# Modulation products in four column groups, a layer norm's normalisation on ScalarE, and a different rhythm of offering its steps

## The chip, the core and the metric

One core of one Trainium2 chip runs the whole program. The metric is the device time of one execution in microseconds. The core has TensorE (PE in the profile), VectorE (DVE), ScalarE (ACT), GpSimd (POOL), and SyncE (SP), which here only issues DMAs. Instructions of one engine run in program order, and an instruction waits on semaphores for what it reads.

## What is computed

One layer of a hybrid block over 1024 tokens and 256 context tokens, D = 2048. Only its first part matters here:

```
m = silu(c) @ w_ada + b_ada                  # shift, scale, gate; 3 x 2048; also for c_ctx
h  = layernorm(x)  * (1 + scale)  + shift    # x: 1024 x 2048
hc = layernorm(xc) * (1 + scale_c) + shift_c # context: 256 x 2048
z  = h @ w_in ;  zc = hc @ w_in              # 6400 columns, cut into the branches
# then an S5 scan, a pooling branch, an RWKV-7 scan, gates, and
x_new = layernorm(alpha * x + gate * (merged @ w_out)) * ln_g + ln_b
```

All of it is in float32. The product `silu(c) @ w_ada` has two rows, one for c and one for c_ctx.

## The kernel before

`phase_ab` computes everything up to the S5 and pooling branches, and `phase_c` the RWKV scan and the output. `phase_ab` has two parts: `adaln` (the first stage) and `in_proj`.

**The first stage.** `adaln` cuts the shift and scale columns of `w_ada` into 128 pieces of 128 x 512 (256 KB each): 4 blocks of 512 columns, for each the scale part and then the shift part, for each part 16 pieces along the contraction. One loop at its end goes over the pieces. It keeps `ARAWS` = 7 pieces in flight through a ring of seven buffers (`ada_load`), and issues an x tile (128 x 2048, 1 MB) after every seventh loaded piece (`x_load`), all on SP's queue. For each piece one product is written: two columns of `sil` as stationary operand, the piece as the moving one, into two partitions of a PSUM tile `ps`. A float32 product is two instructions on PE. After 16 pieces `modulate` copies the two rows out on ACT (`row`), turns them into columns with four small products, and adds the bias on DVE.

**The layer norm.** `layernorm(t, line)` is a generator that runs between the pieces. For each of ten tiles (two of context first): four `bn_stats` and a `bn_aggr` on DVE, a square root on ACT, a reciprocal and the normalisation `(x - mean) * rstd` on DVE, then twice eight transposes on PE, each eight followed by four copies out of PSUM, taken by ACT and DVE in turn. Three such lines run interleaved (`LINES`).

**The operands of the projection.** When all ten tiles are normalised and a block's scale and shift are there, `modulate` goes on for that block: for each of its four groups of 128 features a multiply-add on DVE (`xT`), a rounding copy on ACT (`hi`), a remainder on DVE (`lo`), and the same for the context with two ACT instructions and one on POOL. So there are 16 such steps in all. `in_proj` then starts with feature block 48; it needs the first 256 features for its first step and the last ones for its last.

**What sets the order.** Nothing is scheduled at run time. While the program is written, `Clock` adds up a model of each engine: `note` prices every instruction (`COST` for the three elementwise engines, the number of columns for PE, bytes for DMA) and remembers when each tile is written and read. `Sched.tick(most)` is called between products; it takes up to `most` steps whose due time lies at or before the modelled time of PE, and writes their instructions at this place. `in_proj` uses the same `Sched` and the same `Clock` for all its side work (conv, norms, S5, pooling), with `tick(MOST)` after every projected group. So a price in `COST` changes the program order in all of `phase_ab`. `phase_c` has a planner of its own (`Pace`), which the change doesn't touch.

Most instructions of `phase_ab` are recorded under one line, L300, because a wrapper issues them; they are told apart by the tile names: `ada` (the PSUM tile of the products), `araw` (a piece), `x`, `pm` (transposes; later the projection), `row`, `misc`, `xT`, `hi`, `lo`, `xcT`, `hc_hi`, `hc_lo`. In the late phase, lines 2053 and 2059 are products of 128 rows by 64 columns whose outputs alternate between the two halves of PSUM's partitions: column-tiled products, two groups of 64 columns. Lines 2443 to 2445 are full 128 x 128 products beside them.

Of the kernel before, what the change touches and what calls it, by code (L numbers as in the profile page):

```python
# [9 lines left out]
FT = mybir.dt.float32  # L10
# [13 lines left out]
ALPHA = 2.0 ** 0.25  # L24
AHEAD = 3
ARAWS = 7
LINES = 3
RING = 20
QUOTA = 0.8
# [213 lines left out]
class Clock:  # L243


    LAT = {"tensor": 0.25, "scalar": 0.2, "vector": 0.15, "gpsimd": 0.15}
    COST = {"scalar": (0.17, 0.00075), "vector": (0.08, 0.00105), "gpsimd": (0.1, 0.0022)}

    def __init__(self):
        self.free = dict.fromkeys(("tensor", "scalar", "vector", "gpsimd", "sync", "hwdge", "dma"), 0.0)  # L250
# [3 lines left out]
    def note(self, eng, op, args, kw):  # L254
        aps = [x for x in (*args, *kw.values()) if isinstance(x, bass.AP)]
        if not aps:
            return
        out, ins = aps[0], aps[1:]
        n = math.prod(out.shape[1:])
        o = out.tensor.name  # L260
        who = "dma" if op == "dma_start" else eng
        marks = [self.written.get(x.tensor.name) for x in ins]
        if out.space != DRAM:
            marks += [self.written.get(o), self.read.get(o)]
            if o in self.before:
                p = self.before.pop(o)
                marks += [self.written.get(p), self.read.get(p)]
        t = max([self.free[eng]] + [m[1] for m in marks if m and (m[0] != who or who == "dma")])
        if who == "dma":
            self.free[eng] = t + (1.05 if eng == "gpsimd" else 0.05)  # L270
            t = self.free["hwdge"] = max(t, self.free["hwdge"]) + 0.45
            t = self.free["dma"] = max(t + 0.6, self.free["dma"]) + out.shape[0] * n * 4 / 360e3
            done = t + 1.0
        else:
            if eng == "tensor":
                cost = max(n, 64) * (1 if ins[0].dtype == FR else 2 if op == "transpose" else 4) / 2400
            else:
                a, b = self.COST[eng]
                cost = a + b * n
            t = self.free[eng] = t + cost  # L280
            done = t + self.LAT[eng]
        self.written[o] = who, done
        for x in ins:
            self.read[x.tensor.name] = who, done
        self.last = max(self.last, done)
# [230 lines left out]
def adaln(tc, A, g, const, hb, psA, ap_, raws, hc_hi, hc_lo):  # L516


    nc = tc.nc
    sched = Sched(tc.clock)  # L520
    order = (8, 9, 0, 1, 2, 3, 4, 5, 6, 7)
    x_t, normed = {}, []

    def x_load():
        t = order[len(x_t)]
        x_t[t] = hb.tile([128, D], FT, tag="hb", name=f"x{t}")
        nc.sync.dma_start(x_t[t], A["x"][0, t * 128:(t + 1) * 128, :] if t < 8 else A["ctx"][0, (t - 8) * 128:(t - 7) * 128, :])

    pieces = [(blk, part, k) for blk in range(4) for part in (1, 0) for k in range(16)]
    loaded = []  # L530

    def ada_load():
        blk, part, k = pieces[len(loaded)]
        r = raws.tile([128, 512], FT, name="araw")
        nc.sync.dma_start(r, A["w_ada"][0, k * 128:(k + 1) * 128, part * D + blk * 512:part * D + (blk + 1) * 512])
        loaded.append(r)

    x_load()
    cv, (oc, occ, ob) = load_cols(
        tc, A, g, ap_, psA,  # L540
        [(rows_of(A["c"], 16), 16), (rows_of(A["c_ctx"], 16), 16), (rows_of(A["b_ada"], 48), 48)], "cv")
    ada_load()
    x_load()
    g.sil = sil = const.tile([128, 16, 2], FT, name="sil")
    for i, o in enumerate((oc, occ)):
        nc.scalar.activation(sil[:, :, i], cv[:, o:o + 16], AF.Silu)
    xc_t = ap_.tile([128, 16, TC], FT, name="xcT")
    xT = []
    mod = ap_.tile([128, 16, 2, 2], FT, name="mod")

    def layernorm(t, line):
        while t not in x_t:
            yield
        xt = x_t[t]
        st = ap_.tile([128, 4, 6], FT, name=f"bst{line}", tag=f"bst{line}")
        mv = ap_.tile([128, 4], FT, name=f"mv{line}", tag=f"mv{line}")
        yield
        for i in range(4):
            nc.vector.bn_stats(st[:, i], xt[:, i * 512:(i + 1) * 512])
        nc.vector.bn_aggr(mv[:, 0:2], st)  # L560
        nc.vector.tensor_scalar(mv[:, 2:3], mv[:, 1:2], 1e-6, None, op0=OP.add)
        nc.scalar.activation(mv[:, 3:4], mv[:, 2:3], AF.Sqrt)
        yield
        nc.vector.reciprocal(mv[:, 2:3], mv[:, 3:4])
        nc.vector.tensor_scalar(xt, xt, mv[:, 0:1], mv[:, 2:3], op0=OP.subtract, op1=OP.mult)
        while t < 8 and not {8, 9} <= set(normed):
            yield
        if not xT and t < 8:
            xT.extend(hb.tile([128, 2, T], FT, tag="hb", name=f"xT{i}") for i in range(7))
            xT.append(ap_.tile([128, 2, T], FT, name="xT7"))  # L570
        yield
        for q in range(2):
            ps = psA.tile([128, 8, 128], FT, name="pm", tag="pm", bufs=2)
            for i in range(8):
                k = 8 * q + i
                nc.tensor.transpose(ps[:, i], xt[:, k * 128:(k + 1) * 128], g.ident)
            for b in range(4):
                i = 4 * q + b
                dst = xT[i][:, :, t * 128:(t + 1) * 128] if t < 8 else xc_t[:, 2 * i:2 * i + 2, (t - 8) * 128:(t - 7) * 128]
                copy_on(nc, "dve" if b % 2 else "act", dst, ps[:, 2 * b:2 * b + 2])  # L580
            yield
        normed.append(t)

    def lines(j):
        for t in order[j::LINES]:
            yield from layernorm(t, j)

    g.hi, g.lo, g.made = hi, lo, made = [], [], []

    def modulate(blk, part, ps):  # L590

        row = ap_.tile([2, 512], FT, name="row", tag="row")
        nc.scalar.activation(row, ps[0:2], AF.Copy)
        yield
        pt = psA.tile([128, 512], FT, name="misc", tag="misc", bufs=2)
        for i in range(4):
            nc.tensor.matmul(pt[:, 2 * i:2 * i + 2], row[0:2, i * 128:(i + 1) * 128], g.ident[0:2, 0:2], start=True, stop=True)
        b0 = ob + part * 16 + blk * 4
        m = mod[:, 4 * blk:4 * blk + 4, part, :]
        nc.vector.tensor_tensor(m, pt[:, 0:8].rearrange("p (k m) -> p k m", m=2),  # L600
                                cv[:, b0:b0 + 4].unsqueeze(2).to_broadcast([128, 4, 2]), op=OP.add)
        if part:
            nc.vector.tensor_scalar(m, m, 1.0, None, op0=OP.add)
            return
        yield
        while len(normed) < 10:
            yield
        while len(hi) < 2 * blk:
            yield
        for i in (2 * blk, 2 * blk + 1):  # L610
            h_hi = hb.tile([128, 2, T], FR, tag="hb", name=f"hi{i}")
            h_lo = hb.tile([128, 2, T], FR, tag="hb", name=f"lo{i}")
            hi.append(h_hi)
            lo.append(h_lo)
            for j in range(2):
                k = 2 * i + j
                x, xc = xT[i][:, j], xc_t[:, k]
                nc.vector.tensor_scalar(x, x, mod[:, k, 1, 0:1], mod[:, k, 0, 0:1], op0=OP.mult, op1=OP.add)
                nc.scalar.activation(h_hi[:, j], x, AF.Copy)
                nc.vector.tensor_tensor(h_lo[:, j], x, h_hi[:, j].bitcast(FT), op=OP.subtract)  # L620
                nc.scalar.activation(xc, xc, AF.Identity, scale=mod[:, k, 1, 1:2], bias=mod[:, k, 0, 1:2])
                nc.scalar.activation(hc_hi[:, k], xc, AF.Copy)
                nc.gpsimd.tensor_tensor(hc_lo[:, k], xc, hc_hi[:, k].bitcast(FT), op=OP.subtract)
                if j:
                    made.append(i)
                yield

    for j in range(LINES):
        sched.add(lines(j), 1)
    for n, (blk, part, k) in enumerate(pieces):  # L630
        while len(loaded) < min(n + ARAWS, len(pieces)):
            ada_load()
            if len(loaded) % 7 == 0 and len(x_t) < 10:
                x_load()
        if k == 0:
            ps = psA.tile([128, 512], FT, name="ada", tag="acc", bufs=2)
        nc.tensor.matmul(ps[0:2], sil[:, k, :], loaded[n], start=(k == 0), stop=(k == 15))
        if k == 15:
            sched.add(modulate(blk, part, ps), 0)
        sched.tick()  # L640
    return sched


# [2069 lines left out]
```

## Time and profile before

| | us |
|---|---|
| median of three runs | 2939.46 (2935.54 to 2944.36) |
| the profiled execution's own time | 2930.3 |
| its span, first to last instruction | 2928.4 |
| first stage: last product of a piece ends | 164.2 |
| projection of feature block 48 begins | 167.1 |
| projections end, `phase_c` begins (about) | 1630 to 1680 |

PE is busy 2655.7 us of the span (91%), DVE 1971.3 (67%), POOL 1156.4 (39%), ACT 1033.6 (35%), and the mean granted clock of TensorE is 0.95. A busy share is an average over stages that have different limits, so the stage that the change touches is read by itself: in windows of time, with the DMA rate beside the engines. In the rows, PEld is the load of a stationary operand, SPq is SP's DMA queue, "x36" is a count of instructions merged into one row, and a time in brackets is how long the engine had been idle before.

### The profile page before, as it was taken

The numbers are of one execution on the slowest core, as the hardware profiler recorded it, in microseconds if no ns is written. First come the engines' busy times: TensorE is split into PE (matmuls) and PEld (weight loads), VectorE is DVE, ScalarE is ACT, GpSimd is POOL, SyncE is SP. The second block draws the span as 40 slices with busy tenths as digits, with TensorE's granted clock in tenths as the row PEclk, the third lists the DMA queues.
The fourth block names the chain that finished last, engine by engine and source line by source line (L and its number), as shares of the span: only waits on it lengthen the run. The fifth ranks groups of instructions, "written<-read, shape, count | busy, mean of one in ns | idle before, by whom it ended". The sixth has DMA issues, their size and how long they took to land. (4 is left out here: it accounts for less than half of the span.)

```text
span 2928.4 us, 56400 instructions
## 1 busy us (share of the span) xinstructions
PE 2655.7 (91%) x20080; PEld 2154.8 (74%) x20080; DVE 1971.3 (67%) x4242; ACT 1033.6 (35%) x2611; POOL 1156.4 (39%) x1681
## 2 busy tenths in 40 slices
PE   7989999999999999999899857989988898888786
PEld 2258878888888887778778457877877777777665
DVE  5548235556666567888889466487768775885668
ACT  1321224444444444222222123334444443443223
POOL 0104003343333334322563034455645554566526
PEclk9999999999999999999999978999989899999888
DMA  8834646666666666656443476566766666556754
GB/s 284 265 113 139 152 119 171 167 174 182 176 180 161 168 188 158 168 154 173 128 111 110 128 238 163 156 185 186 188 176 163 173 180 181 141 156 176 247 170 162
DMA packets 698674, 498.49 MB, mean 170 GB/s; under 512 B 347182, under 2 KB 624406, under 8 KB 695574
## 3 DMA queue, kind: packets, MB, share of 16 engines
q1 hardware_dynamic: 672632, 449.52, 55.0%
q0 software_dynamic: 6912, 24.12, 3.0%
q10 hardware_dynamic: 18848, 21.24, 2.1%
q8 instruction: 159, 2.61, 0.4%
q14 instruction: 123, 1.01, 0.1%
HBM read 339.64 MB, written 155.07 MB: 169 GB/s over the span
## 5 line engine op out<-in xcount | busy, mean ns | idle before, releaser
L300 PE MATMUL pm<-hi,whi 128*128 128x512 f32 x1600 | 510.6, 400 | 4.3 <-ACT whi L300 4.2
L300 PE MATMUL pm<-hi,wlo 128*128 128x512 f32 x1600 | 508.1, 399 | 1.9 <-DVE wlo L300 1.9
L300 PE MATMUL pm<-lo,whi 128*128 128x512 f32 x1600 | 508.2, 399 | 0.0
L300 DVE TENSOR_TENSOR wlo<-wraw,whi 128x256 fp32r<-128x256 f32 x400 | 227.2, 574 | 315.4 <-ACT whi L300 288.7
L300 PEld LDWEIGHTS pm<-hi,whi 128*128 128x128 f32 x1600 | 274.2, 189 | 58.1 <-ACT whi L300 6.2
L300 PEld LDWEIGHTS pm<-hi,wlo 128*128 128x128 f32 x1600 | 274.4, 189 | 53.2 <-DVE wlo L300 3.7
L300 PEld LDWEIGHTS pm<-lo,whi 128*128 128x128 f32 x1600 | 274.0, 189 | 50.7 <-issue 2.2
L300 ACT ACTIVATE whi<-wraw 128x256 fp32r<-128x256 f32 x400 | 160.9, 414 | 411.6 <-DMA wraw<-in_w_in 250.6
L2443 PE MATMUL ofacc<-ofhi,ofyh 128*128 128x256 f32 x768 | 252.4, 329 | 23.8 <-DVE ofev L2462 9.8
L2444 PE MATMUL ofacc<-ofhi,ofyl 128*128 128x256 f32 x768 | 225.3, 293 | 1.7 <-POOL ofyl L240 1.7
L2445 PE MATMUL ofacc<-oflo,ofyh 128*128 128x256 f32 x768 | 224.2, 292 | 0.0
L1745 PE MATMUL gp<-spread,kq 128*128 128x128 f32 x1152 | 180.3, 306 | 43.6 <-DVE spread L236 24.4
L1745 PEld LDWEIGHTS gp<-spread,kq 128*128 128x128 f32 x1152 | 155.2, 210 | 55.8 <-DVE spread L236 24.5
L2000 POOL TENSOR_TENSOR faded<-ping,els 64x128 f32<-64x128 f32 x304 | 127.3, 419 | 153.0 <-DVE ping L2005 140.8
L2443 PEld LDWEIGHTS ofacc<-ofhi,ofyh 128*128 128x128 f32 x768 | 154.2, 201 | 41.0 <-DVE ofev L2460 9.6
L240 POOL TENSOR_TENSOR oflo<-ofw,ofhi 128x256 fp32r<-128x256 f32 x145 | 110.1, 759 | 172.2 <-DVE ofhi L236 76.1
L1880 DVE TENSOR_TENSOR tmp<-af,nn 128x31 f32<-128x31 f32 (+15 forms) x310 | 147.0, 474 | 28.4 <-DMA af<-flat 19.6
L2444 PEld LDWEIGHTS ofacc<-ofhi,ofyl 128*128 128x128 f32 x768 | 155.3, 202 | 2.7 <-POOL ofyl L240 2.5
L1882 DVE TENSOR_TENSOR nn<-nn,tmp 128x31 f32<-128x31 f32 (+15 forms) x310 | 148.0, 477 | 10.6
L2445 PEld LDWEIGHTS ofacc<-oflo,ofyh 128*128 128x128 f32 x768 | 154.4, 201 | 0.0
L240 POOL TENSOR_TENSOR ofw<-ofw,ofg 128x256 f32<-128x256 f32 x135 | 108.3, 803 | 87.8 <-DMA ofg<-z_mgate 63.0
L300 POOL TENSOR_TENSOR kd<-kd,kx 128x256 f32<-128x256 f32 x72 | 56.5, 785 | 173.9 <-ACT kd L300 50.3
(513 smaller groups left out, 5547.5 us busy)
## 6 DMA issues: line engine op xcount, KB each, us to landing
wraw<-in_w_in SPq DMA_DIRECT2D x400, 128.0 KB, 2.8
kq<-z_kq SPq DMA_DIRECT2D x80, 512.0 KB, 5.7
araw<-in_w_ada SPq DMA_DIRECT2D x128, 256.0 KB, 3.6
ofw<-in_w_out SPq DMA_DIRECT2D x192, 128.0 KB, 3.6
part<-ofev SPq DMA_DIRECT2D x96, 256.0 KB, 2.7
cds<-z_cd POOLq DMA_DIRECT2D x40, 512.0 KB, 5.3
z_kq<-kq SPq DMA_DIRECT2D x80, 256.0 KB, 3.2
z_kq<-kq SPq DMA_DIRECT2D x160, 128.0 KB, 3.1
```

The costliest lines, as they stand in the source:

```text
L240: (nc.vector if eng == "dve" else nc.gpsimd).tensor_tensor(out, a, b, op=op)
L300: r = x(*args, **kw)
L1745: nc.tensor.matmul(gp[:, i], seg.kb[:, i, :], qb[:, i].rearrange("p h t -> p (h t)"), start=True, stop=True)
L1880: nc.vector.tensor_tensor(tv, af[:, q, q + 1:].unsqueeze(2).to_broadcast([128, nt_, nj]), nn[:, q:q + 1, 0:nj].to_broadcast([128, nt_, nj] ...
L1882: nc.vector.tensor_tensor(nn[:, q + 1:, 0:nj], nn[:, q + 1:, 0:nj], tv, op=OP.subtract)
L2000: nc.gpsimd.tensor_tensor(to[hs], s[hs, :, hs], el[hs].to_broadcast([64, 2, 64]), op=OP.mult)
L2443: nc.tensor.matmul(o, yh[:, sl], whi, start=(first and b == 0), stop=False, skip_group_check=True)
L2444: nc.tensor.matmul(o, yl[:, sl], whi, start=False, stop=False, skip_group_check=True)
L2445: nc.tensor.matmul(o, yh[:, sl], wlo, start=False, stop=last, skip_group_check=True)
```

## The change

Three things are changed in `adaln`, and two prices of the planner with them.

The products of a piece take as stationary operand `wide[:, k]`, 32 columns of which the first two are `sil` and the rest zero, and write 32 partitions of `ps`, those of column group k modulo 4. Each group sums four of the sixteen pieces; `row` copies all 128 partitions, and the small products multiply it by `fours`, a 128 x 2 matrix that adds the four groups. `wide` is zeroed by GpSimd and filled by one DVE copy, and `fours` takes three DVE additions.

The normalisation becomes a tiny DVE instruction (minus mean times rstd) and one ACT instruction, Identity with scale and bias, on the whole tile.

The x tiles are issued after every fifth loaded piece (`XEVERY`), not every seventh, and the steps are offered after every second piece, up to six at once, not up to three after each.

The planner prices a product into 32 partitions at a quarter, and an ACT instruction at 0.2 + 0.00085 us per element, which was 0.17 + 0.00075.

```diff
--- before.py
+++ after.py
@@ -24,6 +24,7 @@
 ALPHA = 2.0 ** 0.25
 AHEAD = 3
 ARAWS = 7
+XEVERY = 5
 LINES = 3
 RING = 20
 QUOTA = 0.8
@@ -244,7 +245,7 @@
 
 
     LAT = {"tensor": 0.25, "scalar": 0.2, "vector": 0.15, "gpsimd": 0.15}
-    COST = {"scalar": (0.17, 0.00075), "vector": (0.08, 0.00105), "gpsimd": (0.1, 0.0022)}
+    COST = {"scalar": (0.2, 0.00085), "vector": (0.08, 0.00105), "gpsimd": (0.1, 0.0022)}
 
     def __init__(self):
         self.free = dict.fromkeys(("tensor", "scalar", "vector", "gpsimd", "sync", "hwdge", "dma"), 0.0)
@@ -274,6 +275,8 @@
         else:
             if eng == "tensor":
                 cost = max(n, 64) * (1 if ins[0].dtype == FR else 2 if op == "transpose" else 4) / 2400
+                if out.shape[0] == 32:
+                    cost /= 4
             else:
                 a, b = self.COST[eng]
                 cost = a + b * n
@@ -544,6 +547,13 @@
     g.sil = sil = const.tile([128, 16, 2], FT, name="sil")
     for i, o in enumerate((oc, occ)):
         nc.scalar.activation(sil[:, :, i], cv[:, o:o + 16], AF.Silu)
+    wide = raws.tile([128, 16, 32], FT, name="wide", bufs=1)
+    nc.gpsimd.memset(wide, 0.0)
+    nc.vector.tensor_copy(wide[:, :, 0:2], sil)
+    fours = ap_.tile([128, 2], FT, name="fours")
+    nc.vector.tensor_tensor(fours, g.ident[:, 0:2], g.ident[:, 32:34], op=OP.add)
+    for j in (64, 96):
+        nc.vector.tensor_tensor(fours, fours, g.ident[:, j:j + 2], op=OP.add)
     xc_t = ap_.tile([128, 16, TC], FT, name="xcT")
     xT = []
     mod = ap_.tile([128, 16, 2, 2], FT, name="mod")
@@ -562,7 +572,8 @@
         nc.scalar.activation(mv[:, 3:4], mv[:, 2:3], AF.Sqrt)
         yield
         nc.vector.reciprocal(mv[:, 2:3], mv[:, 3:4])
-        nc.vector.tensor_scalar(xt, xt, mv[:, 0:1], mv[:, 2:3], op0=OP.subtract, op1=OP.mult)
+        nc.vector.scalar_tensor_tensor(mv[:, 3:4], mv[:, 0:1], -1.0, mv[:, 2:3], op0=OP.mult, op1=OP.mult)
+        nc.scalar.activation(xt, xt, AF.Identity, scale=mv[:, 2:3], bias=mv[:, 3:4])
         while t < 8 and not {8, 9} <= set(normed):
             yield
         if not xT and t < 8:
@@ -589,12 +600,12 @@
 
     def modulate(blk, part, ps):
 
-        row = ap_.tile([2, 512], FT, name="row", tag="row")
-        nc.scalar.activation(row, ps[0:2], AF.Copy)
+        row = ap_.tile([128, 512], FT, name="row", tag="row")
+        nc.scalar.activation(row, ps, AF.Copy)
         yield
         pt = psA.tile([128, 512], FT, name="misc", tag="misc", bufs=2)
         for i in range(4):
-            nc.tensor.matmul(pt[:, 2 * i:2 * i + 2], row[0:2, i * 128:(i + 1) * 128], g.ident[0:2, 0:2], start=True, stop=True)
+            nc.tensor.matmul(pt[:, 2 * i:2 * i + 2], row[:, i * 128:(i + 1) * 128], fours, start=True, stop=True)
         b0 = ob + part * 16 + blk * 4
         m = mod[:, 4 * blk:4 * blk + 4, part, :]
         nc.vector.tensor_tensor(m, pt[:, 0:8].rearrange("p (k m) -> p k m", m=2),
@@ -630,14 +641,16 @@
     for n, (blk, part, k) in enumerate(pieces):
         while len(loaded) < min(n + ARAWS, len(pieces)):
             ada_load()
-            if len(loaded) % 7 == 0 and len(x_t) < 10:
+            if len(loaded) % XEVERY == 0 and len(x_t) < 10:
                 x_load()
         if k == 0:
             ps = psA.tile([128, 512], FT, name="ada", tag="acc", bufs=2)
-        nc.tensor.matmul(ps[0:2], sil[:, k, :], loaded[n], start=(k == 0), stop=(k == 15))
+        c = 32 * (k % 4)
+        nc.tensor.matmul(ps[c:c + 32], wide[:, k], loaded[n], start=(k < 4), stop=(k >= 12))
         if k == 15:
             sched.add(modulate(blk, part, ps), 0)
-        sched.tick()
+        if k % 2:
+            sched.tick(6)
     return sched
```

## Rows read from the trace of the kernel before

**Rows 1.** Windows of 100 us: span, busy time by engine (count), clock, DMA share, GB/s.

```profile
600.00:700.00 100.00, 100.00 (x532) 83.87 (x532) 60.66 (x136) 46.40 (x133) 38.53 (x51) 1.00 0.65 179
...
1400.00:1500.00 100.00, 87.74 (x428) 72.39 (x426) 89.11 (x110) 19.90 (x37) 57.37 (x41) 0.95 0.41 114
```

**Rows 2.** The first stage in steps of 10 us, same columns.

```profile
10.00:20.00 10.00, 9.07 (x17) 1.58 (x18) 6.54 (x17) 0.61 (x3) 0.00 (x0) 1.00 1.01 389
20.00:30.00 10.00, 9.56 (x39) 3.33 (x37) 5.78 (x10) 1.92 (x5) 0.00 (x0) 1.00 0.93 321
```

**Rows 3.** Three stretches of the first stage, same columns.

```profile
38.00:42.00 4.00, 1.77 (x10) 0.69 (x9) 3.80 (x8) 0.54 (x3) 0.00 (x0) 1.00 0.89 304
42.00:46.00 4.00, 3.86 (x18) 2.33 (x16) 2.93 (x6) 1.60 (x5) 0.00 (x0) 0.59 0.43 167
...
106.00:164.00 58.00, 58.00 (x158) 14.05 (x156) 27.28 (x29) 24.52 (x39) 9.88 (x12) 1.00 0.82 265
```

**Rows 4.** Instruction groups of 0 to 200 us by form: count, busy us, mean ns, idle.

```profile
L300 PE MATMUL ada<-araw,sil 128*2 128x512 f32 x256 | 118.6, 610 | 2.1 <-DMA araw<-in_w_ada 1.4 <-ACT sil L300 0.7
...
L300 DVE TENSOR_TENSOR lo<-xT,hi 128x1024 fp32r<-128x1024 f32 x16 | 19.6, 1225 | 18.0 <-ACT hi L300 18.0
...
L300 DVE TENSOR_SCALAR xT<-xT,mod 128x1024 f32<-128x1024 f32 x16 | 17.0, 1065 | 0.1
L300 ACT ACTIVATE hi<-xT 128x1024 fp32r<-128x1024 f32 x16 | 16.9, 1057 | 26.3 <-DVE xT L300 26.3
L300 DVE TENSOR_SCALAR x<-x,mv 128x2048 f32<-128x2048 f32 x10 | 13.5, 1346 | 0.4
...
L300 ACT ACTIVATE xcT<-xcT,mod 128x256 f32<-128x256 f32 x16 | 9.4, 585 | 0.0
```

**Rows 5.** DMA of 0 to 165 us: total, then issues: count, size, time to landing.

```profile
DMA packets 20152, 44.25 MB, mean 268 GB/s; under 512 B 2272, under 2 KB 2480, under 8 KB 18864
...
araw<-in_w_ada SPq DMA_DIRECT2D x128, 256.0 KB, 3.6
```

**Rows 6.** Timeline of PE: start us, length us, engine, line, what, count.

```profile
23.90 0.86 PEld L300 LDWEIGHTS pm<-ident,x 128*128 128x128 f32 x8 [0.86 <-issue]
...
41.72 3.15 PE L300 MATMUL pm<-ident,x 128*128 128x128 f32 x16 [2.23 <-DVE x L300]
...
107.54 1.05 PE L300 MATMUL misc<-ident,row 2*128 2x2 f32 x8
...
108.52 15.61 PE L300 MATMUL ada<-araw,sil 128*2 128x512 f32 x36
```

**Rows 7.** Timeline of SP's DMA queue in the first stage.

```profile
82.97 0.38 SPq L300 DMA_DIRECT2D x<-in_x  x1
83.45 75.38 SPq L300 DMA_DIRECT2D araw<-in_w_ada  x72
```

**Rows 8.** Timeline: the first operand step, and the end of the first stage.

```profile
104.04 0.80 DVE L300 TENSOR_SCALAR xT<-xT,mod 128x1024 f32<-128x1024 f32 x1
...
164.35 0.59 ACT L300 ACTIVATE row<-ada 2x512 f32<-2x512 f32 x1 [13.00 <-PE ada L300]
...
167.14 0.74 PE L300 MATMUL pm<-hi,whi 128*128 128x512 f32 x2 [2.89 <-ACT whi L300]
...
189.80 0.32 PE L300 MATMUL misc<-ident,e 56*128 56x56 f32 x1 [7.38 <-DMA e<-in_rwkv_r_k]
```

**Rows 9.** Timeline of PE late in the kernel: column-tiled products and their neighbours.

```profile
2000.90 0.45 PE L2053 MATMUL banku<-uv,kbn 128*64 128x64 f32 x8
2001.18 0.40 PE L2059 MATMUL banky<-uv,ar 128*64 128x64 f32 x8
2001.52 0.39 PE L2443 MATMUL ofacc<-ofhi,ofyh 128*128 128x256 f32 x1
2001.74 0.28 PE L2444 MATMUL ofacc<-ofhi,ofyl 128*128 128x256 f32 x1
2001.86 0.27 PE L2445 MATMUL ofacc<-oflo,ofyh 128*128 128x256 f32 x1
```

## The prediction, made before the changed kernel was run

> **What bounds the kernel now.** The windows of the whole span come first. From 500 to 1100 us PE is busy all the time at a clock of 1.00, [rows 1] shows one of those six windows: what is saved ahead of it should come through to the end, because nothing there waits for anything but PE. Later, in 1400 to 1500, PE is at 88% and DVE at 89%: there the order of side work costs PE some 12 us. The change itself lies in the first stage, which ends at 164.2 us, just ahead of the ACT copy `row` of [rows 8].
>
> In that stage the reader should hold PE against DMA. From 106 to 164 us PE is busy in all 58 us, while the DMA share is 0.82 at 265 GB/s [rows 3]. The pieces there are a stream of back-to-back instructions: 36 of them in 15.61 us [rows 6], 0.434 us each, and a piece is two, 0.867 us. SP's queue shows the same from the other side: the 72 issues after the last x tile took 75.38 us, 1.05 us each [rows 7], because an issue waits until PE has released one of seven buffers. So PE sets the pace of the DMA. Early on, with seven fresh buffers, the same queue moved 389 GB/s at a share of 1.01, then 321 at 0.93 [rows 2].
>
> PE's account up to 164.2 us: 128 pieces x 0.867 = 111 us; transposes, 20 groups of eight at 0.86 us = 17; small products, eight groups at 1.05 us = 8 [rows 6]. That is 136 of the 156 us after the first product at 8 us. The rest is stalls. The clearest: PE waits 2.23 us for a normalised x, and its 16 transposes then take 3.15 us at half speed [rows 6]. The granted clock falls to 0.59 behind a stretch in which PE was busy 1.77 of 4 us, and the DMA share falls to 0.43 as buffers stay held [rows 3].
>
> **Products in column groups.** A piece stays two passes of 0.434 us; new is that neighbouring pieces lie in different column groups. The trace has no 32-column stream with 512 moving columns. The nearest rows are column-tiled products with 64 moving columns in two groups: eight instructions start within 0.28 us, 0.035 us each [rows 9], where 64 columns at the price of the ada rows (0.434 / 512 x 64) would take 0.054 one after another. The overlap is 1.55 or, if about 0.008 us of that is a fixed cost per instruction, the full 2. With four groups it could reach 4, but the second pass of a piece needs the group of its first pass, and instructions start in program order; so I take neighbours overlapping, 0.434 us a piece. The bounds are 0.217 (all four overlap) and 0.867 (none). At 0.434 PE needs 56 + 17 + 8 = 81 us.
>
> The rows also show a cost of switching. After the column-tiled run the first two full products start 0.22 us apart, the next 0.12 [rows 9]: 0.1 us a switch. Twenty transpose groups and eight small groups, each entered and left, are 56 switches, 5.6 us of PE, which is not the bound any more. The Trainium skill speaks against the change here: "TensorEngine Tiling (Array Packing)", Key Properties, says that changing the tiling mode drains the engine. The trace agrees, with 0.1 us; a drain alone leaves the sum as it is.
>
> **DMA takes over.** The stage moves 44.25 MB [rows 5], before and after. What rate holds? Rate divided by share gives 323 GB/s in the late stretch [rows 3], 345 in 20 to 30 us and 385 in 10 to 20 us [rows 2]. I take 334, the middle of the lower two, since the highest was a burst. The ring allows it: landing 3.6 us [rows 5], two passes 0.87, about 0.5 for the next issue, 5.0 us for seven pieces, or 369 GB/s. So 44.25 / 0.334 = 132.5 us, about 4 us before data flows and 1 us from the last landing to the last product's end: 138 us instead of 164. The bounds: at 385 GB/s 120 us; at PE's old pace, below.
>
> **Normalisation on ACT, x tiles earlier.** DVE loses ten instructions of 1.346 us and gains ten tiny ones. ACT gains ten of 2.1 us, twice the 1.057 us of 1024 elements, up to 2.4 if the scale and bias cost what 0.585 us for 256 elements suggests [rows 4]. ACT is busy 24.5 of 58 us late in the stage [rows 3] and has room. On the chain of one tile this adds 0.8 to 1.1 us plus a semaphore. Behind the waiting ACT instruction the copies out of PSUM are queued, and behind those the next transposes, which hold PE and so the pieces. Seven pieces cover some 5 us; without that cover ten tiles would cost up to 10 us. I take 2. Eight x issues move ahead of up to 16 pieces in SP's queue; the bytes are the same, and the last x tile now comes after 40 pieces, 21 MB, and lands at about 67 us; it was issued at 83 [rows 7]. Offering every second piece delays a step by half a piece and bunches transposes; it is in the same 2 us. Zeroing `wide`, its copy and `fours` come ahead of the first product, perhaps 1 us; the queue is still filling then, nothing.
>
> **What comes next in line.** The sixteen steps of the operands are each a chain of 1.065 (DVE) + 1.057 (ACT) + 1.225 (DVE) = 3.35 us [rows 4]. The first of them began at 104 us [rows 8], 21 behind the last x issue. That issue now comes near 62, so the steps begin near 83, and twelve take 40: done at 123, ahead of 140, so the last block still starts when its modulation is there. If one step is left over, 3.4 us; I take 1. The waits behind the stage (wraw, 2.9 us; the load of r_k, 7.4 us [rows 8]) stay.
>
> **The price of ACT in the planner** changes the order of all of `phase_ab`. The new price of 256 elements is 0.42 us, the old 0.36. Where PE is full this is worth nothing; of the five windows from 1100 to 1600 us PE loses 12 us to waits in the worst [rows 1] and 26 in all, and a new order may win or lose a part. I take 0, and 8 us either way.
>
> **The sum.** 164.2 - (138 + 2) = 24, less 1: 23 us. On the profiled execution, 2930.3 us of its own (span 2928.4 and 1.9 around it), that is 2907; it ran 9 us below the median of the runs, 2939.5, and from the median it is 2916. 0.3%, about what a measurement of this kernel can tell from no change, is 9 us.
>
> **Rivals.**
> A, the forecast: DMA bounds the stage. With 120 to 146 us for it and 8 us of order, 2901 to 2926. Chance 0.62.
>
> B, the clock. PE gets 1.2 GHz (0.5 in the rows) in part of the stage, since it now has gaps. For it: the only deep fall in the stage came behind a stretch with PE at 1.77 of 4 us [rows 3]. Against it: a piece alone holds its group 0.87 us and the next comes after 0.78, so some group always streams. At half clock with an overlap of 2 a piece costs 0.867 again. If only the 88 pieces behind the last x tile pay this, with the old stretch's 0.92 us each, small products included, they take 67 to 148 us; if it is the whole stage, 2 x 81 + 8 = 170. So 2923 to 2945, middle 2930. Chance 0.15. The Trainium skill has the rule, "TensorE: Matmul & The Clock Gate", Part 1: the throttled state is the default and activity releases it. The trace agrees as far as [rows 3] go; no row shows what 32 columns count for.
>
> C, the change doesn't do what it says: no overlap at full clock. Then PE pays 0.867 a piece, but x comes earlier and the early stalls shrink: 67 + 88 x 0.92 = 148, with stalls 155. 2930. Against it: [rows 9]. Chance 0.07.
>
> D, slower: half clock all through, and the overlap only 1.55. A piece then costs 2 x 0.867 / 1.55 = 1.12 us, and the stage 8 + 143 + 34 + 17 = 202 us, 38 later: 2977. At this clock it decides from an overlap below 2.1: 111 us / (0.5 x overlap) must fit into 156 - 51 = 105 us. Chance 0.05.
>
> E, the new order in the projections gives back the gain in the stretch after 1100 us, where PE already idles: 20 us more of waits there, 2936 to 2945. For it: DVE at 89% [rows 1]. Chance 0.11.
>
> **How the numbers follow.** Faster by over 0.3%: nearly all of A (0.61), half of B (0.08), half of C (0.04), a little of E: 0.74. Slower by over 0.3%: D, a third of E, a tenth of B: 0.10. Within: 0.16. The range runs from A's best, 2901, to where B and C lie and E begins, 2938; D, most of E and A's far end stay outside.
>
> **What would show it.** Right: DMA share above 0.9 at 320 to 350 GB/s from 10 to 135 us; `ada` rows starting about 0.4 us apart where several pieces wait; the last product of a piece near 140, the projection near 143; from 500 us on the same picture 23 us earlier. Wrong: a granted clock near 0.5 between 70 and 140 us (B, D); `ada` instructions 0.43 us apart throughout (C); a stage 24 us shorter but projections that end no earlier (E). I would be wrong above all if the rate of 334 GB/s doesn't hold behind stalls of the norm.

## The result: the first stage came in as forecast, and the kernel is slower

| kernel | median us | runs | ratio to before |
|---|---|---|---|
| before | 2938.68 | 2935.54 to 2944.36 | 1 |
| after | 2973.31 | 2968.57 to 2980.02 | 1.013 [1.011, 1.015] |

The changed kernel is 34.6 us slower, where 23 us faster was forecast. Its profiled execution took 2968.57 us of its own, with a span of 2966.5, 38.1 above the span before. Where do 38.1 us come from? The views of single tiles give the landmarks. Each row has the shortest, median and longest duration in ns, then the first and the last start in us. Before:

```profile
L300 PE MATMUL pm<-hi,whi x1600: 387/392/799, 167.1 to 1635.9; 128*128 128x512 f32 x178
...
L300 SPq DMA_DIRECT2D kx<-z_kx x40: 480/607/1819, 421.1 to 1154.1; - x40
...
L300 PE MATMUL misc<-plu,wpl x16: 590/592/697, 1450.8 to 1638.8; 128*128 128x512 f32 x16
...
L1745 PE MATMUL gp<-spread,kq x1152: 272/275/582, 1691.5 to 2703.8; 128*128 128x128 f32 x192
```

After:

```profile
L303 PE MATMUL pm<-hi,whi x1600: 387/393/799, 147.0 to 1641.4; 128*128 128x512 f32 x178
...
L303 SPq DMA_DIRECT2D kx<-z_kx x40: 483/734/1222, 409.7 to 1314.4; - x40
...
L303 PE MATMUL misc<-plu,wpl x16: 590/1046/1193, 1610.0 to 1723.1; 128*128 128x512 f32 x16
...
L1758 PE MATMUL gp<-spread,kq x1152: 270/275/584, 1734.1 to 2742.0; 128*128 128x128 f32 x192
...
L303 PE MATMUL ada<-araw,wide x256: 589/617/1063, 9.0 to 143.5; 128*32 128x512 f32 x128
```

The reader should subtract in four parts. The projections (`pm<-hi,whi`) begin at 147.0 and not at 167.1: 20.1 us gained. From their first to their last product they take 1494.4 us and not 1468.8: 25.6 lost. From the last one to the first `gp`, where `phase_c` begins, it is 92.7 us and not 55.6: 37.1 lost. `phase_c` itself is 4.5 shorter. -20.1 + 25.6 + 37.1 - 4.5 = 38.1.

The two other rows show what was late. `kx` is loaded once in each of the 40 turns of the loop that prepares keys and decays for the scan. Its 39 gaps took 733.0 us before, 18.8 a turn, and 904.7 after, 23.2 a turn. The work that stands behind it in the queue (the gate, S5, pooling, GLU) is pushed back: the pooling's last product (`misc<-plu,wpl`) comes 81.7 us after the last projection, before 2.9.

Windows of before tell what kind of work this is. The columns are those of [rows 1]: span, busy time and count of PE, PEld, DVE, ACT, POOL, then clock, DMA share, GB/s.

```profile
500.00:1100.00 600.00, 600.00 (x3180) 502.51 (x3179) 366.21 (x835) 278.92 (x784) 224.17 (x296) 1.00 0.65 176
1100.00:1640.00 540.00, 512.52 (x2465) 420.12 (x2463) 453.07 (x662) 147.41 (x283) 206.61 (x177) 0.98 0.52 143
...
1637.00:1691.00 54.00, 34.56 (x71) 13.74 (x69) 14.78 (x13) 7.69 (x10) 1.55 (x4) 0.81 0.46 144
```

And of after, the last one again from the end of the projections to `phase_c`:

```profile
500.00:1100.00 600.00, 588.93 (x3084) 493.26 (x3085) 310.00 (x755) 248.16 (x690) 171.93 (x238) 1.00 0.56 154
1100.00:1640.00 540.00, 507.65 (x2479) 417.81 (x2478) 450.07 (x710) 184.16 (x382) 239.18 (x223) 0.98 0.56 150
...
1642.00:1734.00 92.00, 45.25 (x81) 16.78 (x79) 47.04 (x40) 7.69 (x10) 7.31 (x8) 0.70 0.48 163
```

From 500 to 1100 us, where PE hid everything, DVE now does 310 us of work and not 366. So 56 us of side work moved out of the stretch in which it cost nothing. The stretch behind is no fuller for it: there DVE was at 453 of 540 us already and is at 450 now. It takes on 48 more instructions of DVE (710 and 662), but long ones leave it at its end: 32 us turn up behind the projections (47.0 and 14.8), where PE is busy half of the time. In the stretch that [rows 1] show, 600 to 700 us, PE was busy 100.00 us and is busy 98.37.

The end of that tail is a chain on DVE. The timeline of after, start and length in us, idle time and releaser in brackets:

```profile
1695.31 0.69 DVE L303 COPY plr<-plu 128x1024 f32<-128x1024 f32 x1 [8.32 <-DMA plu<-z_pm]
1696.03 2.16 DVE L303 TENSOR_TENSOR plr<-plr 128x1920 f32<-128x1920 f32 x1
...
1701.20 5.80 DVE L303 TENSOR_TENSOR plr<-plr 128x1856 f32<-128x1856 f32 x3
...
1719.11 1.23 DVE L303 TENSOR_TENSOR plu<-plinv,plu 128x1024 f32<-128x1024 f32 x1
```

On PE, in the same view, the pooling product that waits for it:

```profile
1689.51 10.89 PE L303 MATMUL misc<-gluy,wglu 128*128 128x512 f32 x25
1720.43 3.73 PE L303 MATMUL misc<-plu,wpl 128*128 128x512 f32 x4 [20.03 <-issue]
```

PE stands 20.0 us before it. The releaser is given as "issue", but the product's operand `plu` is written by the DVE instruction at 1719.11, so the wait is DVE's.

**The first stage.** The windows of after, beside [rows 2] and [rows 3]:

```profile
10.00:20.00 10.00, 7.70 (x16) 1.45 (x16) 7.46 (x18) 0.41 (x2) 0.00 (x0) 1.00 1.03 411
20.00:30.00 10.00, 7.07 (x43) 3.32 (x38) 2.68 (x11) 7.96 (x9) 0.00 (x0) 1.00 0.95 349
60.00:70.00 10.00, 7.51 (x36) 4.14 (x36) 4.17 (x13) 5.69 (x7) 0.00 (x0) 0.66 0.34 111
106.00:140.00 34.00, 31.79 (x110) 8.29 (x108) 18.98 (x22) 16.89 (x28) 6.58 (x8) 1.00 0.95 326
...
8.00:140.00 132.00, 107.97 (x463) 39.42 (x464) 72.49 (x156) 61.19 (x101) 8.23 (x10) 0.96 0.88 317
```

Late in the stage the DMA share is 0.95 at 326 GB/s, and was 0.82 at 265, and PE now waits 13.7 us for pieces, before 1.4: DMA is the bound there, as forecast. There is one hole, from 60 to 70 us, where the timeline of PE shows a wait for a normalised x:

```profile
62.49 1.97 PE L303 MATMUL pm<-ident,x 128*128 128x128 f32 x8 [4.78 <-ACT x L303]
```

The groups by form of 0 to 200 us, which answer to [rows 4], have the new instructions (count, busy us, mean ns, idle):

```profile
L303 PE MATMUL ada<-araw,wide 128*32 128x512 f32 x256 | 83.7, 671 | 13.7 <-DMA araw<-in_w_ada 13.7
L303 ACT ACTIVATE x<-x,mv 128x2048 f32<-128x2048 f32 x10 | 20.7, 2091 | 4.6 <-DVE mv L303 4.5
```

### The profile page after: what moved, and what is told of

It is laid out like the page before. It is cut to its first block, busy times and chain, and to the rows that moved or that the text cites. A ratio compares the mean times of both kernels' runs of the same rounds, so it can differ in the third digit from the quotient of the medians.

```text
span 2966.5 us, 56406 instructions
## 1 busy us (share of the span) xinstructions
PE 2638.4 (89%) x20080; PEld 2160.7 (73%) x20080; DVE 1926.3 (65%) x4246; ACT 1062.4 (36%) x2629; POOL 1147.6 (39%) x1682
## 5 line engine op out<-in xcount | busy, mean ns | idle before, releaser
L303 DVE TENSOR_TENSOR wlo<-wraw,whi 128x256 fp32r<-128x256 f32 x400 | 209.3, 531 | 303.0 <-ACT whi L303 280.6
L2013 POOL TENSOR_TENSOR faded<-ping,els 64x128 f32<-64x128 f32 x304 | 127.2, 418 | 150.1 <-DVE ping L2018 137.9
L303 POOL DMA_DIRECT2D cds<-z_cd x40 | 23.2, 579 | 282.1 <-PE misc L303 271.2
```

Source lines behind the costliest of these rows:

```text
L303: r = x(*args, **kw)
L2013: nc.gpsimd.tensor_tensor(to[hs], s[hs, :, hs], el[hs].to_broadcast([64, 2, 64]), op=OP.mult)
```

## The experiments

The first theory: the first stage brings some 23 us, and the new price of ACT in the planner alone costs about 60. The rivals: the new order of the stage itself upsets the projections, or an engine's longer instructions do. All kernels were timed in three rounds beside the kernel before. "Gain" is the median of before on the same chip less that of the kernel. The four times are read as above from the tile views and add up to the span. They are of one execution each. After and e11 have the same first stage, and so have e1 and e12, yet their projections begin at 147.0 and 150.6, and at 144.0 and 142.1: a difference of under 4 us there says little. `phase_c`, the last time, is the same program in all and takes 1227.1 to 1246.2.

| kernel | median | ratio | gain | projections begin | they last | then to `gp` | to the end |
|---|---|---|---|---|---|---|---|
| before | | | | 167.1 | 1468.8 | 55.6 | 1236.9 |
| after | 2973.31 | 1.013 [1.011, 1.015] | -34.6 | 147.0 | 1494.4 | 92.7 | 1232.4 |
| e1_oldprice | 2908.96 | 0.9903 [0.9879, 0.9927] | 26.8 | 144.0 | 1473.2 | 56.2 | 1236.1 |
| e2_newprice_alone | 2986.04 | 1.0175 [1.0152, 1.0197] | -50.3 | 165.2 | 1491.3 | 90.6 | 1232.5 |
| e3_price_174 | 2955.58 | 1.0074 [1.0052, 1.0096] | -19.8 | 144.8 | 1491.4 | 85.0 | 1230.7 |
| e4_prodold | 2963.74 | 1.01 [1.0084, 1.0116] | -28.0 | 147.4 | 1473.3 | 101.7 | 1246.0 |
| e5_onegroup | 2928.34 | 0.9979 [0.9963, 0.9995] | 5.8 | 162.0 | 1473.5 | 55.5 | 1235.1 |
| e6_dvenorm | 2915.04 | 0.9931 [0.9908, 0.9955] | 19.1 | 148.5 | 1476.6 | 56.3 | 1231.8 |
| e7_tick1 | 2932.63 | 1.000 [0.9985, 1.0014] | 1.6 | 167.6 | 1467.8 | 56.2 | 1239.1 |
| e8_x7 | 2921.8 | 0.9964 [0.995, 0.9978] | 12.4 | 154.2 | 1471.5 | 56.1 | 1238.3 |
| e9_bnprice_tick1 | 2918.7 | 0.9953 [0.9938, 0.9967] | 13.8 | 151.7 | 1472.1 | 55.1 | 1238.8 |
| e10_bnprice | 2916.62 | 0.9951 [0.9933, 0.9969] | 15.9 | 148.7 | 1471.5 | 55.4 | 1239.2 |
| e11_newprice_nogate | 2934.09 | 1.0019 [1.0001, 1.0037] | -1.6 | 150.6 | 1483.7 | 61.8 | 1246.2 |
| e12_oldprice_nogate | 2870.35 | 0.9791 [0.976, 0.9821] | 62.2 | 142.1 | 1479.5 | 12.8 | 1227.1 |

### The price undone, and the price alone

After with the old price:

```diff
-    COST = {"scalar": (0.2, 0.00085), "vector": (0.08, 0.00105), "gpsimd": (0.1, 0.0022)}
+    COST = {"scalar": (0.17, 0.00075), "vector": (0.08, 0.00105), "gpsimd": (0.1, 0.0022)}
```

> The changed kernel with one thing undone: the planner prices an ACT instruction at 0.17 + 0.00075 us per element again. Theory 1 (the new price alone reorders the side work of the projections and makes the RWKV operand loop, the one that loads kx, fall behind; the rest of the change gains): the last kx load comes near 1138 us, 16 before the kernel before, the projection runs 16 us ahead throughout, and the time is 16 to 22 us below the kernel before, 2917 to 2923. Theory 2 (the ACT normalisation, the x order or the bunched steps of the first stage cost the time): 2960 to 2975 as in the changed kernel.

Before with the new price, the same lines the other way round:

> The kernel before with only the new ACT price, 0.2 + 0.00085, nothing else of the change. Theory 1: the first stage stays at 164 us, the kx loads stretch from 723 us in all to about 890, and the time is the changed kernel's plus the 16 to 20 us that its first stage gains: 2985 to 2995. Theory 2: 2939, as before.

e1 is 26.8 us faster than before, 4 us more than Theory 1 allowed, and e2 50.3 slower. One line of the planner, which changes no instruction but only the order in which they are written, is worth 61 us on the new stage (26.8 + 34.6) and 50 on the old. On the old stage, in e2, DVE's work from 500 to 1100 us falls just as in after:

```profile
500.00:1100.00 600.00, 588.57 (x3084) 492.45 (x3082) 308.79 (x747) 245.25 (x682) 172.81 (x237) 0.99 0.56 153
```

The rows of e1 have the old shape. Its windows:

```profile
8.00:140.00 132.00, 108.91 (x470) 39.83 (x470) 74.20 (x158) 63.16 (x102) 9.05 (x11) 0.97 0.89 320
500.00:1100.00 600.00, 600.00 (x3178) 502.41 (x3178) 365.24 (x842) 280.40 (x788) 222.75 (x291) 1.00 0.65 174
```

And its loop and its products, in the views of the tiles:

```profile
L303 SPq DMA_DIRECT2D kx<-z_kx x40: 495/610/1456, 399.6 to 1132.6; - x40
...
L303 PE MATMUL ada<-araw,wide x256: 589/617/1063, 8.4 to 140.5; 128*32 128x512 f32 x128
```

PE is at 600.00 of 600 again, DVE at 365 of the 366 us of before, and 39 turns take 733.0 us, as before. The first stage looks a little better than in after: the hole at 60 to 70 us has closed in part (222 GB/s there, in after 111), and the last product starts at 140.5. e1 beats both kernels, and it is the change as it was forecast: the edits of the stage at a price of 0 for the new order.

### A smaller step of the price

```diff
-    COST = {"scalar": (0.2, 0.00085), "vector": (0.08, 0.00105), "gpsimd": (0.1, 0.0022)}
+    COST = {"scalar": (0.174, 0.00075), "vector": (0.08, 0.00105), "gpsimd": (0.1, 0.0022)}
```

> As e1, but the fixed part of the ACT price is 0.174 and not 0.170 us: 4 ns more per instruction. Theory 1a (the loop keeps a rhythm with the other side work, and any price that makes a due time miss its offer breaks it): almost the whole loss comes back, the last kx load near 1280 us, time 2955 to 2975. Theory 1b (the loss grows with the price, 0.174 has 2 to 3% of the step to the new price at 256 elements and 13% of its fixed part): at most 5 us above e1.

4 ns more on each ACT instruction than in e1 cost 46.6 us (26.8 + 19.8), three quarters of the whole loss. The loop again takes long, `kx` from 398.4 to 1277.1, 22.5 us a turn. So the loss isn't proportional to the price: the loop keeps its rhythm at 0.17 and has lost it at 0.174. This run doesn't show what breaks it.

### The loop priced as of old, the rest new

```diff
...
-                a, b = self.COST[eng]
+                a, b = (0.17, 0.00075) if eng == "scalar" and self.cheap else self.COST[eng]
...
-            yield from production()
+            it = production()
+            while True:
+                tc.clock.cheap = True
+                x = next(it, "end")
+                tc.clock.cheap = False
+                if x == "end":
+                    break
+                yield x
```

> The changed kernel with the new ACT price, except for the instructions of production(), the loop that loads kx, which keep the old price. Theory 1c (the loop falls behind because its own chain is priced longer): the loop is back to some 18 us a turn, time 2920 to 2930. Theory 1d (it falls behind because it and the other users of the two PSUM buffers called misc no longer come in the same rhythm, whoever's price moved): a turn stays at 22 us, time 2960 to 2980.

Of the 61 us at most 7 come back, and the loop stays slow, `kx` from 410.0 to 1300.8, 22.8 us a turn. The projections last 1473.3 us, as in e1, but the tail grows to 101.7. So the loop doesn't need a new price of its own to be slow; the new price of the others' instructions does it. How they hold it up in the plan wasn't isolated and stays open. Two places of the planner could: its steps ask for the `misc` buffers in PSUM, which all side work shares, and `tick` offers nothing while ACT or DVE is modelled over 6 us ahead of PE (`LIMIT`), which a price reaches directly. No run tells them apart.

### The four column groups

e1 with every product in group 0 (`row` and the small products are cut to the same 32 partitions, which isn't shown):

```diff
-        c = 32 * (k % 4)
-        nc.tensor.matmul(ps[c:c + 32], wide[:, k], loaded[n], start=(k < 4), stop=(k >= 12))
+        c = 0
+        nc.tensor.matmul(ps[c:c + 32], wide[:, k], loaded[n], start=(k == 0), stop=(k == 15))
```

> e1 (the changed kernel at the old ACT price) with all products of a piece in one column group: 32 columns as there, but the same 32 partitions for all sixteen pieces; the prices, and so the program order, are e1's. Theory A (the groups overlap, and with them PE stops being what the DMA waits for): without them a piece costs 0.87 us of PE again, the last product of a piece ends at 155 to 165 us, not at 141, and the time is 2924 to 2936. Theory B (the gain comes from the earlier x tiles and the lighter DVE): 2905 to 2915, as e1.

e5 came out as Theory A has it: it loses 21 us of e1's 26.8, and its projections begin 18 us later. Runs of products that stood ready show the overlap itself. The timeline of e5, one group, two instructions to a piece:

```profile
27.72 3.62 PE L303 MATMUL ada<-araw,wide 128*32 128x512 f32 x8
...
32.29 1.90 PE L303 MATMUL ada<-araw,wide 128*32 128x512 f32 x4
...
42.33 1.04 PE L303 MATMUL ada<-araw,wide 128*32 128x512 f32 x2
```

After, four groups:

```profile
29.07 1.33 PE L303 MATMUL ada<-araw,wide 128*32 128x512 f32 x8
...
31.36 1.05 PE L303 MATMUL ada<-araw,wide 128*32 128x512 f32 x4
...
40.56 1.05 PE L303 MATMUL ada<-araw,wide 128*32 128x512 f32 x2
```

And e1, four groups, where four pieces stand ready together:

```profile
80.41 1.07 PE L303 MATMUL ada<-araw,wide 128*32 128x512 f32 x8
```

One piece takes 1.04 to 1.05 us in both. Two take 1.90 in one group and 1.05 in two. Four take 3.62 in one group and 1.07 in four, hardly more than one piece does; in the row of after at 29.07 the fourth starts 0.29 us behind the others, and they take 1.33. So not only neighbours overlap but all four pieces, 3.4 times (3.62 / 1.07). The Trainium skill, "TensorE: Matmul & The Clock Gate", Part 3, has a measured 2.38 times for three column tiles with 512 columns; this trace shows 3.4 times for four, in float32.

### The other parts, each undone on e1

The normalisation back on DVE:

```diff
-        nc.vector.scalar_tensor_tensor(mv[:, 3:4], mv[:, 0:1], -1.0, mv[:, 2:3], op0=OP.mult, op1=OP.mult)
-        nc.scalar.activation(xt, xt, AF.Identity, scale=mv[:, 2:3], bias=mv[:, 3:4])
+        nc.vector.tensor_scalar(xt, xt, mv[:, 0:1], mv[:, 2:3], op0=OP.subtract, op1=OP.mult)
```

> e1 with the normalisation back on DVE, one instruction of 1.35 us as in the kernel before. Theory A (ACT makes each tile's chain 0.8 to 1.1 us longer, PE waits for it, and DVE has room): the first stage ends up to 5 us earlier than e1's, 2903 to 2909. Theory B (DVE is crowded in the first 100 us and the move relieves it): 2912 to 2920.

The steps offered after every piece:

```diff
-        if k % 2:
-            sched.tick(6)
+        sched.tick()
```

> e1 with the steps offered after every piece, up to three, as in the kernel before. If the rhythm of two pieces bunches transposes and stalls PE: 2900 to 2908. If it saves switches between column groups and full products: 2911 to 2918. If neither matters: 2906 to 2912.

The x tiles at their old distance:

```diff
-XEVERY = 5
+XEVERY = 7
```

> e1 with an x tile after every seventh piece, as in the kernel before. The bytes are the same; the last x tile comes some 16 pieces, 11 us, later, and the operand steps behind it too. If these steps (twelve of 3.4 us before the last block) become the bound: the projection starts up to 8 us later, 2912 to 2918. If the stage stays bound by DMA: 2906 to 2912.

e6's time lies in Theory B's range, 8 us behind e1, but the intervals of the two overlap. Its projections begin 4.5 us later, and 1.8 of these stand ahead of its first product (10.2, in e1 8.4), which waits for the first load when no tile has been normalised yet. PE waits less for x in it, 1.9 us where e1 has 6.0. So a gain by the move to ACT isn't shown, nor that DVE was crowded. The other two missed. e8 gives back 14 us, 2 more than its worst case: PE's waits for the operand steps (`xT`) grow from 1.9 to 7.5 us, and the projections begin 10 us later. e7 gives back 25, all of the gain but 1.6, with projections that begin at 167.6, no earlier than before. Undoing each of three parts costs 21 + 25 + 14 = 60 us, over twice what all give together (26.8): they need each other. The waits of PE in 0 to 165 us show what e7 lacks (total, times, longest):

```profile
PE pm L303 <- ACT x L303: 17.3, 4, 8.2
PE ada L303 <- DMA araw<-in_w_ada: 15.0, 16, 2.9
```

PE's queue holds transposes whose x is not normalised yet, and the pieces behind them can't be released. In e1 these waits are 6.0 us in all, the longest 1.5.

### Why the offers matter

The transposes are written too early if the planner takes the norm for shorter than it is. The timeline of after has the instruction that it misjudges:

```profile
67.94 0.68 DVE L303 BATCH_NORM_STATS2 bst<-x 128x6 f32<-128x512 f32 x1
```

The planner prices it by its output, six numbers: 0.08 + 0.00105 x 6 = 0.086 us, where 0.68 is measured. e9 is e7 with that price put right, e10 is e1 with it:

```diff
-        n = math.prod(out.shape[1:])
+        n = math.prod((ins[0] if op == "bn_stats" else out).shape[1:])
```

> e7 (old ACT price, steps offered after every piece) with one more price changed: the planner prices bn_stats by the 512 elements it reads, 0.62 us, not by the 6 it writes, 0.09. Theory A (e7 lost 23 us because the planner takes a tile for normalised 2 us too early, writes its transposes too early and PE waits for ACT; offers after two pieces hid that by being late): PE's waits for x in the first stage fall from 17 us to under 6, the last product of a piece ends near 141 us, 2906 to 2914. Theory B (the offers after each piece cost by switching between column groups and full products): 2926 to 2934 as e7.

> e1 (old ACT price, offers after two pieces) with bn_stats priced by the 512 elements it reads. Theory A: the 6 us that PE still waits for x in e1 shrink, the last product of a piece ends at 137 to 141 us, 2903 to 2909. Theory B (with the later offers the price is already absorbed): 2908 to 2914.

The waits of PE in e9:

```profile
PE ada L303 <- DMA araw<-in_w_ada: 18.1, 18, 3.3
...
PE pm L303 <- ACT x L303: 1.8, 1, 1.8
```

The waits for x fall from 17.3 to 1.8 us, as Theory A has it, and 12 of the 25 us come back; the time stays 5 us above its range, and the last product starts at 148.3 and not near 141. With that price right, offering every second piece is worth 2 us (e10 against e9, 15.9 and 13.8), which these intervals can't tell from nothing; with it wrong, 25 (e1 against e7). So half of what e7 loses hangs on the wrong price, and the offers make up for that. The rest isn't explained, and e10 missed: the right price alone makes e1 11 us slower and not faster; its waits for pieces grow from 8.2 to 21.7 us, and its projections begin 4.7 us later. Why is open.

### The gate left out, at either price

After and e1 without the gate's 64 loads and 64 DVE instructions in the projections:

```diff
-        todo = [(n, k) for n in range(4) for k in range(16)]
+        todo = []
```

> The changed kernel, new ACT price, without the 64 loads and multiply-adds that make the gate of the modulation: the gate is then the bias alone, and that part of the result is left out. They run between the RWKV operand loop and the pooling branch on DVE. Theory A (the loop's lateness pushes the pooling branch past the last projection, and some 37 us of the loss are this tail): pooling ends under the projections, from the last projection to the first product of phase_c it is 56 us as in the kernel before, not 93, and the time is 2925 to 2937. Theory B (the tail is the S5 branch's or the memory's, not the pooling's): the tail stays above 85 us, 2960 or more.

> The same left out at the old ACT price, the control for e11: there the pooling branch ends under the projections anyway. The tail stays at 56 us; only DVE's 48 us less work in the projections can show: 2900 to 2909.

Both kernels leave the gate's products out of the result. The gate is 45 to 51 us of DVE's busy time (after less e11, e1 less e12) that stands in the queue ahead of the pooling and the GLU. With the new price the tail falls from 92.7 to 61.8 us without it: the pooling's last product starts at 1622.7, ahead of the last projection (1634.3), which bears out that its backlog on DVE makes the long tail. The control missed: with the old price the tail was to stay at 56, and it fell to 12.8. What stands in that tail is the GLU, in the views of before and of e12:

```profile
L300 PE MATMUL misc<-gluy,wglu x64: 592/592/1222, 1639.3 to 1680.0; 128*128 128x512 f32 x64
...
L303 PE MATMUL misc<-gluy,wglu x64: 591/592/593, 1575.6 to 1629.2; 128*128 128x512 f32 x64
```

In before the GLU's 64 products begin behind the last projection (1635.9), in e12 under the projections, which end at 1621.6. DVE isn't what holds them up there: it is busy 14.8 of 54 us in the tail of before and 13.5 of 61.8 in that of e11, and waits for ACT and DMA itself. So each tail is side work that comes late, in after the pooling too, and the 55.6 us of before were no floor. The price still costs 64 us between the two (62.2 + 1.6), as much as with the gate: leaving the gate out shortens the backlog, but the slow loop ahead of it stays (`kx` to 1317.0 in e11, to 1130.3 in e12).

## Why the prediction was wrong, step by step

**The step that failed** is "The price of ACT in the planner": "I take 0, and 8 us either way". Measured, it is 61 us on the new stage (e1 against after) and 50 on the old (e2). It had taken the size from PE's idle time, 26 us in five windows from 1100 us on, some part of which a new order may win or lose. That is what a better order could win in those windows. What a worse one can lose depends on the side work that lies under a busy PE and can slip out from under it: DVE 366 us in 500 to 1100, of which 56 slipped. [rows 1] had the warning, DVE at 89% in 1400 to 1500: a stretch that can take little on. Why the loop falls behind at the new price stays open. "Where PE is full this is worth nothing" is true of the time in that stretch and false of the end.

**Rival E** was the mechanism: a shorter stage, and projections that end no earlier (last one at 1641.4, before 1635.9). Its price was 20 us of waits, all within the projections. Within them it was 25.6; the tail, 37.1 us, was in no rival: the stretch between the projections and `phase_c` stands in no step of the prediction.

**DMA takes over**: right. The stage was to end at 140; its last product starts at 143.5 in after and 140.5 in e1. The rate was to be 334 GB/s: 317 over 8 to 140 us in after and 320 in e1, with 326 late in the stage. 44.25 MB at 317 take 139.6 us and not 132.5, with the 5 us at the two ends 144.6, and the last product of after ends at 144.1; the hole at 60 to 70 us is part of that lower rate. The stage was to bring 23 us without the price: the projections of e1 begin 23.1 us earlier, and its time is 26.8 lower. That they agree so well is partly luck, since the rate came lower, and the offers and the x tiles' distance are worth more than they were costed at. Rivals B, C and D, 0.27 together, didn't come: the granted clock is 0.96 in the stage, and the pieces overlap. The span of rival A, 2901 to 2926, doesn't come out of its own bounds: around 2916, a stage of 120 to 146 us and 8 us of order give some 2890 to 2930. The measured time lies outside either.

**Products in column groups**: right that they overlap, too small a factor: 0.434 us a piece was forecast, four together take 1.07, 0.27 each and less when the fixed part of a run is left off. The step assumed that a second pass blocks its neighbours. It changes little in the sum, because DMA sets the pace. The 0.1 us that the prediction reads as a switch is hardly one. The same timeline of before has the same two products behind full 128 x 128 ones, where no tiling changes:

```profile
1999.59 0.66 PE L2226 MATMUL misc<-ident,gvn 128*128 128x128 f32 x4
2000.01 0.37 PE L2443 MATMUL ofacc<-ofhi,ofyh 128*128 128x256 f32 x1
2000.21 0.28 PE L2444 MATMUL ofacc<-ofhi,ofyl 128*128 128x256 f32 x1
```

They start 0.20 us apart there, and 0.22 behind the column-tiled run [rows 9].

**Normalisation on ACT**: 2.1 us was forecast for one instruction, 2.09 measured; PE's waits for it are 8.3 us in after and 6.0 in e1, before 6.6 for DVE's. It costed the move at up to 2 us; e6 shows no such cost, and no gain clear of its interval. "Offering every second piece ... is in the same 2 us" was mis-sized most: undone it costs 25 us (e7). The x tiles' distance, of which only the earlier finish was counted, costs 14 (e8).

**What comes next in line**: right in its outcome. The projection starts 3.5 us behind the last product (147.0 - 143.5, and 3.5 in e1), as before (3.4), and PE waits the same 2.9 us for `whi`. The steps were late: the first began at 98.4 us in after and 91.1 in e1, not near 83, and the twelfth at 150.1 and 139.3, where it was to be done at 123. It cost nothing.

## What to carry to other kernels

Where an order is fixed ahead of time by a model with prices, a change of a price can be a change of the whole program, as here: bound it by the side work that a full engine covers and the next stretch can't take on, not by the idle time that is there, and time it by itself (e2) before it goes in with anything else. A price nearer to the measured duration isn't safer: 0.418 us for 256 elements is nearer to the 0.414 us of the rounding copies (`whi`, in the page of after) than the 0.362 of before, and loses 50 us. And read the stretch behind the bound engine's last instruction too; here 55.6 us lay there, and 12.8 were left once the gate's DVE work was out of the queue (e12).

## What the runs showed of TensorE that was not expected

The passes of two float32 products in different column groups start together, and no second pass stands between them. The timeline of e1, two pieces, in a window of its first 0.12 us and then in one up to its end:

```profile
83.38 0.62 PE L303 MATMUL ada<-araw,wide 128*32 128x512 f32 x2
...
83.38 1.05 PE L303 MATMUL ada<-araw,wide 128*32 128x512 f32 x4
```

Of a single piece in after, in a window of its first 0.34 us:

```profile
40.56 0.62 PE L303 MATMUL ada<-araw,wide 128*32 128x512 f32 x1
```

Two instructions are under way at once where two pieces stand ready, one where there is one, and the other pass follows in both. So two pieces end 1.05 us after they start, as one does, and four end 1.07 us after (the row at 80.41 above). Whether the instructions are written in that order or start out of order isn't in the trace.
